# A hybrid decoder layer on one core: the second norm's row products moved from VectorE to ScalarE and GpSimd, its sums moved into PSUM banks

## The chip, the cores and the metric

One core of a Trainium2 chip runs the whole layer. TensorE (PE) multiplies into PSUM, VectorE (DVE), ScalarE (ACT) and GpSimd (POOL) work on tiles in SBUF and, the first two, in PSUM; SyncE (SP) issues most transfers. The metric is the device time of one launch in microseconds, as the median of several runs.

## The reference

The layer works on 1024 rows (the sequence) of 1024 float32 values. Cut to what matters here:

```
h  = rms_norm(x, mix_norm);  z = h @ w_in
o_gla = gated linear attention of part of z, RMS-normed per head and gated
o_swa = sliding-window attention with sinks of the rest of z
x  = x + concat([o_gla, o_swa]) @ w_out
h2 = rms_norm(x, ffn_norm)            # x * rsqrt(mean(x*x) + eps) * gain, row by row
u  = causal_dwconv(h2 @ w_up, conv_w, conv_b);  a, b = split(u)
out = x + (silu(a) * b) @ w_down
```

The change lies in the stretch from `@ w_out` to the first products of `h2 @ w_up`.

## The kernel before

**Numbers and products.** Float32 accuracy is had from a faster format: each operand is kept as a high part (rounded, `F32R`) and a low part (the value less the high part). `split` makes them: ScalarE copies the high part, GpSimd (or the engine named) subtracts. A product takes three passes, high by high, high by low, low by high, so a 128x512 output over 512 inner values is twelve matmuls.

**Seven products for eight.** Each large product is a 2x2 block product done in a Strassen-like scheme of seven block products P1 to P7 on sums and differences of blocks. Row tiles are 128 rows; tile `t` and tile `t + 4` are the upper and lower half of a block pair. Several products may go onto the same bank: `onto` in `o_product` says which. For `w_out`, P6, P5 and P3 go onto P1's bank, and after each the bank is added to a part of the residual rows `acc` (line 838, in `o_adds`, VectorE). P7 and P4 have banks of their own: P7 is added to both halves of `acc[i + 4]`, P4 to half 0 of it.

**Second norm.** When `acc[t]` is whole, after P3 for `t < 4` and after P4 for `t >= 4`, these steps follow:

- `norm2_stat(t)`: ScalarE squares `acc[t]` with a running sum (line 213). The squares themselves are not used; they are written into `h`, the buffer of the normed rows (`n2h`, two buffers). VectorE and GpSimd turn the sum into the row's factor `r` (lines 176 and 178).
- `norm2_rows(t)`: VectorE computes `h = acc * r * gain` in two halves (line 219).
- `norm2_tr(t)`: TensorE transposes `h` into two banks (eight 128x128 transposes). For `t < 4` (line 274, in `tr_hi`) ScalarE writes the high parts into `big`, a copy `b11` of the first half's transposes is kept, and low parts follow: the first half's on GpSimd from `b11` for `t < 3` (line 229), the rest on VectorE (line 286). For `t >= 4` (line 240) the banks are left to the next step.
- `norm2_sums(t)`, `t >= 4`: VectorE forms the differences and sums that the Strassen scheme of the next product wants: T1 = p0 - b11, T3 = p1 - b12, T2 = p1 + b11 (line 262, into the second half of `h`), T4 = b21 - T2 + ... (lines 264 and 265), each split into `big` or `ex[0..2]`. T2's low part goes to GpSimd, the others to VectorE.

**Order.** The program is a list of events, each with a time in units of about 5.2 us (`at`, `at_us`; `O` is the start of the `w_out` products, `TU` = `O` + 14 the start of the `w_up` products). Events are sorted by that time and issued. From `O` to `TU`, TensorE's order is fixed to be that of the list. On VectorE, ScalarE, GpSimd and SP the framework orders the instructions by priority and by its own estimate of when they are ready; each engine then works strictly in that order on the chip. The products of the last part run P2, P3, P4 for pair 0, then P2 and P3 for 1, P7 for 2, P4 for 1, and so on to P7 and P4 for pair 3; the transposes stand between them, at `O + 0.5 * n` for the tile's `n`.

**First chunks of the next product.** `w_up` is read in 22 chunks of channels with two sides each (`load_side`, into three `raw` buffers). Chunk 0's operands are split or summed during the stretch (`first_sums`, lines 910 to 918, VectorE), and also A11 and A12 of chunk 1. After tile 3's transposes come chunk 0's P1 and P2, tile 7's transposes, chunk 1's P1 and P2, then chunk 0's P3 (operand S4), P5 and P6. Chunk 1's other sums (lines 910 to 912) are on GpSimd.

**Gate transposes.** `gate_tr(7)` (line 667), the last of the linear attention's gated outputs, stands among the first `w_out` products.

Of the kernel before, what the change touches and what calls it, by code (L numbers as in the profile page):

```python
# [9 lines left out]
F32 = mybir.dt.float32  # L10
F32R = mybir.dt.float32r
I32 = mybir.dt.int32
AF = mybir.ActivationFunctionType
# [4 lines left out]
P = 128  # L18
T = 1024
D = 1024  # L20
NT = T // P
KD = D // P
# [6 lines left out]
SUMS, EA, EB = 2.01, -25, -14  # L29
# [5 lines left out]
def hymba_layer_kernel(ctx, tc, x, mix_norm, w_in, w_alpha2, b_alpha, gla_norm,  # L35
# [3 lines left out]
    act, dve, pool, pe, sp = nc.scalar, nc.vector, nc.gpsimd, nc.tensor, nc.sync  # L39
# [30 lines left out]
    def raw_tile(name):  # L70
        return base.tile([P, 1024], F32, tag="raw", name=name, bufs=RAW_BUFS)
# [109 lines left out]
    halves = (slice(0, 512), slice(512, D))  # L181
# [22 lines left out]
    def norm1(t):  # L204
        for i in range(2):
            norm1_mul(t, i)
        norm1_stat(t)

    def norm2_stat(t):
        pn, acc = fin["pn"], fin["acc"][t]  # L210
        h = fin["h", t] = pn.tile([P, D], F32, tag="n2h", name=f"n2h_{t}", bufs=2)
        ss = pn.tile([P, 1], F32, tag="n2ss", name=f"n2ss_{t}", bufs=2)
        act.activation(h, acc, AF.Square, accum_out=ss)
        fin["r", t] = rms_scale(ss, D, 1, f"n2{t}", pn, "n2")

    def norm2_rows(t):
        h, acc, r = fin["h", t], fin["acc"][t], fin["r", t]
        for c in halves:
            dve.scalar_tensor_tensor(h[:, c], acc[:, c], r[:, 0:1], fin["ffn"][:, c],  # L219
                                     op0=ALU.mult, op1=ALU.mult)  # L220

    def norm2_tr(t):
        h = fin["h", t]
        if t < 4:
            b11 = fin["b11"] = fin["pn"].tile([P, 4, 2, P // 2], F32, tag="b11", name=f"b11_{t}", bufs=1)
            tr_hi(t, 0, h, "n2", True)
            act.copy(b11, trs["n2", t, 0])
            if t < 3:
                pool.tensor_sub(tr_dst(t, 0, 1, True), b11, tr_dst(t, 0, 0, True).bitcast(F32))
            else:  # L230
                tr_lo(t, 0, "n2", True)
            tr_hi(t, 1, h, "n2", True)
            tr_lo(t, 1, "n2", True)
            return
        pbs = fin["pb", t] = []
        for q in range(2):
            pt = bank(f"n2pt_{t}_{q}")
            for k in range(4):
                c = (q * 4 + k) * P
                pe.transpose(pt[:, k * P:(k + 1) * P], h[:, c:c + P], ident)  # L240
            pbs.append(pt.rearrange("p (k c h) -> p k h c", k=4, h=2))

    def norm2_sums(t):

        i, ex = t - 4, fin["ex"]
        p0, p1 = fin["pb", t]

        def put(src, dst, eng=dve):
            dst = dst.rearrange("p k r (h c) -> p k r h c", h=2)
            split(src, dst[:, :, 0], dst[:, :, 1], eng)  # L250

        b12 = fin["h", t][:, 0:512].rearrange("p (k h c) -> p k h c", k=4, h=2)
        b11 = fin["b11"]
        b21 = big[:, i, 4:8].bitcast(F32).rearrange("p k r (h c) -> p k r h c", h=2)
        act.copy(b12, p0)
        put(p1, big[:, t, 4:8])
        dve.tensor_sub(p0, p0, b11)
        put(p0, big[:, t, 0:4])
        dve.tensor_sub(p1, p1, b12)
        put(p1, ex[1][:, i])  # L260
        t2 = fin["h", t][:, 512:].rearrange("p (k h c) -> p k h c", k=4, h=2)
        dve.tensor_add(t2, p1, b11)
        put(t2, ex[0][:, i], pool)
        dve.tensor_sub(p0, b21[:, :, 0], t2)
        dve.tensor_add(p0, p0, b21[:, :, 1])
        put(p0, ex[2][:, i])

# [12 lines left out]
    def tr_dst(t, q, r, parted):  # L280
        dst = big[:, t, q * 4:q * 4 + 4, r, :]
        return dst.rearrange("p k (h c) -> p k h c", h=2) if parted else dst

    def tr_lo(t, q, tag, parted=False):
        hi, lo = (tr_dst(t, q, r, parted) for r in range(2))
        dve.tensor_sub(lo, trs[tag, t, q], hi.bitcast(F32))
# [10 lines left out]
    raws = {}  # L297
# [366 lines left out]
    def gate_tr(t, gs):  # L664
        pb = bank(f"ogt{t}")
        for h in range(4):
            pe.transpose(pb[:, h * P:(h + 1) * P], gs[:, h * P:(h + 1) * P], ident)
        pv = pb.rearrange("p (h c) -> p h c", h=4)
        g32, l32 = (a[:, t, :].rearrange("p (j c) -> p j c", j=4) for a in (vg[0], qo))
        hi, lo = big[:, t, 0:4, 0, :], big[:, t, 0:4, 1, :]  # L670
        act.activation(hi, pv, AF.Copy, scale=glan)
        dve.scalar_tensor_tensor(lo, pv, glan, hi.bitcast(F32), op0=ALU.mult, op1=ALU.subtract)
        if t < 4:
            act.activation(g32, pv, AF.Copy, scale=glan)
            split(l32, big[:, t, 4:8, 0, :], big[:, t, 4:8, 1, :])
            return
        i = t - 4
        dve.scalar_tensor_tensor(pv, pv, glan, l32, op0=ALU.mult, op1=ALU.subtract)
        s2 = fin["ex"][1][:, (i + 2) % 4]
        split(pv, s2[:, :, 0], s2[:, :, 1], dve)  # L680
        split(l32, big[:, t, 4:8, 0, :], big[:, t, 4:8, 1, :])
        dve.tensor_add(qo[:, i, :], pb, qo[:, i, :])
        dve.tensor_sub(vg[0][:, i, :], vg[0][:, i, :], pb)
# [5 lines left out]
    fin = {}  # L689
# [60 lines left out]
    psb = {}  # L750
# [64 lines left out]
        sp.dma_start(fin["acc"][t], x[t * P:(t + 1) * P, :])  # L815

    def o_product(name, i):
        onto = "P1" if name in ("P6", "P5", "P3") else None
        if onto is None:
            psb["o", name, i] = bank(f"o{name}_{i}")  # L820
        pb = psb["o", onto or name, i]
        left = o_left(name, i)
        for k in range(4):
            for n, (ra, rb) in enumerate(PASSES):
                pe.matmul(pb, lhsT=left[:, k, ra, :], rhs=two_streams(ow[name, k][:, rb, :]),  # L825
                          start=(onto is None and k == 0 and n == 0), stop=(k == 3 and n == 2),
                          skip_group_check=onto is not None)

        if (name, i) not in (("P7", 0), ("P7", 1)):
            o_adds(name, i, pb)  # L830

    def o_adds(name, i, pb=None):
        if pb is None:
            pb = psb["o", name, i]
        for dt, half in {"P1": ((0, 0),), "P6": ((4, 0),), "P5": ((4, 1),), "P3": ((0, 1),), "P2": ((0, 0),),
                         "P7": ((4, 1), (4, 0)), "P4": ((4, 0),)}[name]:
            part = fin["acc"][i + dt][:, half * 512:half * 512 + 512].rearrange("p (h c) -> p h c", h=2)
            dve.tensor_add(part, part, halves_of(pb))
        if name in ("P3", "P4"):
            norm2_stat(i + 4 if name == "P4" else i)  # L840
# [52 lines left out]
        dve.tensor_copy(cc, pcc[:, 0:176].rearrange("p (a b) -> p a b", a=4))  # L893

    def load_side(ch, sd):
        raw = raws["u", ch, sd] = raw_tile(f"up{ch}_{sd}").rearrange("p (k n) -> p k n", k=KD)
        c0 = sd * DFF + ch * P
        sp.dma_start(raw, w_up[:, c0:c0 + P].rearrange("(k p) n -> p k n", p=P))

# [296 lines left out]
    def at(time, f, *a):  # L1196
        ev.append((time, len(ev), f, a))
# [45 lines left out]
    TQ, TK, TV, TG, TR, TO = 0.0, 8.0, 12.8, 20.8, 28.8, 36.8  # L1243
# [67 lines left out]
    for t in range(NT):  # L1311
        s = 11.0 + 1.9 * t
        at(s - (0.7 if t == 4 else 0.3), swa_qt, t)
        at(s + 1.0, swa_scores, t, 0)
        at(s + 1.6, swa_scores, t, 1)
        at(s + 3.2, swa_pt, t, 0)
        at(s + 3.8, swa_pt, t, 1)
        at(s + 4.9, swa_pv, t)
        s = TG + t
        at(s - 2.4, gla_lh, t)  # L1320
        at(s - 1.4, gla_exp, t)
        at(s + 1.0, gla_tr, t)
        if t < NT - 1:
            if t:
                at(s + 1.75, gla_mid, t + 1)
            at(s + 1.8, gla_state, t)
        at(s + 1.9, gla_a, t)
        at(s + 2.7, gla_o, t)
        at(TR + t + 1.3 if t < 7 else O + 0.75, lambda tt=t: gate_tr(tt, psb.pop(("r", tt))))
    at(TR + 2.0, open_acc)  # L1330
    for k2 in range(2):
        at(TR + 1.6 + 0.05 * k2, load_local, k2)
# [26 lines left out]
    for n, (name, i) in enumerate((("P2", 0), ("P3", 0), ("P4", 0), ("P2", 1), ("P3", 1), ("P7", 2), ("P4", 1), ("P2", 2),  # L1359
# [3 lines left out]
        if name in ("P3", "P4"):  # L1363
            t = i + 4 if name == "P4" else i
            at(u + 0.005, norm2_rows, t)
    for t, n in ((0, 19), (4, 20), (1, 22), (5, 24), (2, 26), (6, 27), (3, 28)):
        at(O + 0.5 * n - 0.002, norm2_tr, t)
        if t > 3:
            at(O + 0.5 * n + 0.01, norm2_sums, t)
    at(TU - 7.994, mark)  # L1370
    def at_us(us, f, *a):
        at(TU + us / 5.2, f, *a)
# [39 lines left out]
    at_us(1.8, open_ff)  # L1412
    at_us(starts[2, 0] - 0.05, open_down_banks)
    at_us(-42, load_chunk, 0)
    at_us(-41, load_side, 1, 0)
    for (ch, op), us in (((0, "A11"), EA), ((0, "A12"), EB), ((1, "A11"), -9.8), ((1, "A12"), -9.7),
                         ((0, "S4"), 1.74), ((0, "S1"), 1.75), ((0, "S2"), 1.77), ((0, "S3"), 1.9),
                         ((0, "A22"), 1.91)):
        at_us(us, *((behind,) if us < 0 and ch else ()), up_operand, ch, op)
# [73 lines left out]
```

## Time and profile before

| | us |
|---|---|
| runs: median (lowest to highest, 3 runs) | 999.76 (999.27 to 1000.34) |
| the profiled execution's own time | 1001.43 |
| its span, first to last instruction | 999.7 |
| TensorE busy | 974.2 |
| VectorE busy | 825.3 |
| GpSimd busy | 647.5 |
| ScalarE busy | 500.0 |

The span is what the profile's rows are measured in; the profiled execution is 1.7 us longer than its span and 0.17% above the median. A busy TensorE is not TensorE at its peak, as matmuls are pipelined. A wait on TensorE's row names the engine and line that released it. All times in rows are microseconds from the first instruction, unless a column is said to be nanoseconds.

### The profile page before, as it was taken

Reading aid. Unit: us, or ns where it says so; the run is one execution under the profiler, and the core shown is the slowest. Engines: PE = TensorE matmul, PEld = TensorE weight load, DVE = VectorE, ACT = ScalarE, POOL = GpSimd, SP = SyncE. Lnnn points to the kernel's source line nnn. Section 1 sums busy time; section 2 is a strip of 40 time slices with the busy share of each in tenths; the row PEclk is TensorE's granted clock in tenths of the full one; section 3 lists DMA queues with packets and bytes.
Section 4 is the critical chain, followed back from the end, with each engine's and each line's share of the span. In section 5 each row is a group of like instructions: output and inputs, shape, how many; then the busy total and the mean of one; then the engine's idle time right before and its main releaser. Section 6 shows DMA issues by size and latency. Waiting matters only on the chain.

```text
span 999.7 us, 13937 instructions
## 1 busy us (share of the span) xinstructions
PE 974.2 (97%) x4915; PEld 842.5 (84%) x4915; DVE 825.3 (83%) x1368; ACT 500.0 (50%) x1029; POOL 647.5 (65%) x539
## 2 busy tenths in 40 slices
PE   8999999999999978999999999999999999999998
PEld 6888887888888766878888888888888888888887
DVE  6877767767565798698999989898989899898986
ACT  5637655445454354455454545545454545455451
POOL 5592132335575424787879788887888788978750
PEclk9999999999999997999999999999999999999999
DMA  7152223131305101212121221212120212222104
GB/s 228 62 154 70 46 57 87 27 86 64 106 1 189 43 0 43 85 43 64 43 64 42 64 63 50 77 43 85 43 85 22 66 42 63 64 63 64 43 22 169
DMA packets 67541, 68.23 MB, mean 68 GB/s; under 512 B 4651, under 2 KB 52238, under 8 KB 67471
## 3 DMA queue, kind: packets, MB, share of 16 engines
q1 hardware_dynamic: 63484, 62.35, 20.4%
q10 hardware_dynamic: 3986, 4.99, 2.1%
q8 instruction: 39, 0.64, 0.3%
q14 instruction: 32, 0.25, 0.1%
HBM read 58.41 MB, written 4.19 MB: 63 GB/s over the span
## 4 chain that ended last, share of the span: by engine, by line
PE 77%; DVE 9%; POOL 5%; issue 3%; DMA 2%; ACT 2%; ACTq 0%; SPq 0%; POOLq 0%; DVEq 0%
PE fb L976 35%; PE dn_P L1157 17%; PE dg L348 4%; PE dr L348 4%; PE dv L348 3%; PE oP L825 3%; PE pv L534 1%; DVE n2h L219 1%; PE dl L1186 1%; PE fb L1186 1%; PE dq L848 1%; DMA up<-in_w_up_dram 1%; PE go L644 1%; PE ga L635 1%; DMA wob<-in_w_out_dram 1%
## 5 line engine op out<-in xcount | busy, mean ns | idle before, releaser
L1157 PE MATMUL dn_P<-dw,dg 128*128 128x512 f32 x840 | 205.2, 381 | 1.4 <-DVE acc L1161 0.7
L1161 DVE TENSOR_TENSOR acc<-acc,dn_P 128x1024 f32<-128x1024 f32 x140 | 169.3, 1210 | 31.3 <-PE dn_P L1157 31.2
L1157 PEld LDWEIGHTS dn_P<-dw,dg 128*128 128x128 f32 x840 | 157.2, 189 | 27.8 <-DVE acc L1161 3.2
L107 POOL TENSOR_TENSOR dw<-dn,dw 128x512 fp32r<-128x512 f32 x50 | 64.6, 1292 | 35.6 <-ACT dw L104 35.6
L983 DVE SCALAR_TENSOR_TENSOR ua<-fb,cc,ua 128x511 f32<-128x511 f32 (+1 forms) x84 | 61.9, 739 | 1.2 <-ACT ua L988 0.8
L976 PE MATMUL fb<-big,A11w 128*128 128x512 f32 x252 | 58.3, 380 | 1.1 <-ACT e L1032 1.1
L976 PE MATMUL fb<-big,S1w 128*128 128x512 f32 x252 | 58.6, 379 | 0.0
L976 PE MATMUL fb<-big,A12w 128*128 128x512 f32 x252 | 58.1, 379 | 0.0
L976 PE MATMUL fb<-big,S4w 128*128 128x512 f32 x252 | 58.1, 379 | 0.0
L976 PE MATMUL fb<-ex,S2w 128*128 128x512 f32 x252 | 58.0, 379 | 0.0
L976 PE MATMUL fb<-ex,S3w 128*128 128x512 f32 x252 | 57.8, 379 | 0.0
L976 PE MATMUL fb<-ex,A22w 128*128 128x512 f32 x252 | 57.8, 379 | 0.0
L510 POOL TENSOR_TENSOR pr<-pr,sm 128x512 f32<-128x512 f32 x16 | 17.3, 1080 | 61.4 <-DVE sm L509 36.0
L988 ACT ACTIVATE ua<-fb,cc 128x512 f32<-128x512 f32 x42 | 32.7, 778 | 46.6 <-DVE fb L1036 30.1
L976 PEld LDWEIGHTS fb<-big,A11w 128*128 128x128 f32 x252 | 47.5, 189 | 8.2 <-ACT e L1032 1.5
L976 PEld LDWEIGHTS fb<-big,A12w 128*128 128x128 f32 x252 | 47.6, 189 | 6.8
L976 PEld LDWEIGHTS fb<-ex,S2w 128*128 128x128 f32 x252 | 47.6, 189 | 6.8
L976 PEld LDWEIGHTS fb<-ex,S3w 128*128 128x128 f32 x252 | 47.6, 189 | 6.8
L976 PEld LDWEIGHTS fb<-big,S4w 128*128 128x128 f32 x252 | 47.6, 189 | 6.8
L976 PEld LDWEIGHTS fb<-ex,A22w 128*128 128x128 f32 x252 | 47.6, 189 | 6.8
L976 PEld LDWEIGHTS fb<-big,S1w 128*128 128x128 f32 x252 | 47.6, 189 | 6.8
L107 POOL TENSOR_TENSOR A22w<-up,A22w 128x512 fp32r<-128x512 f32 x22 | 30.0, 1364 | 31.6 <-ACT A22w L104 31.6
(487 smaller groups left out, 2571.8 us busy)
## 6 DMA issues: line engine op xcount, KB each, us to landing
up<-in_w_up_dram SPq DMA_DIRECT2D x44, 512.0 KB, 3.8
dn<-in_w_down_dram SPq DMA_DIRECT2D x22, 512.0 KB, 3.5
acc<-in_x_dram SPq DMA_DIRECT2D x8, 512.0 KB, 4.8
out_dram<-acc SPq DMA_DIRECT2D x15, 256.0 KB, 2.1
xt<-in_x_dram SPq DMA_DIRECT2D x7, 512.0 KB, 3.3
vraw<-in_w_in_dram SPq DMA_DIRECT2D x4, 512.0 KB, 3.9
graw<-in_w_in_dram SPq DMA_DIRECT2D x4, 512.0 KB, 4.0
qt<-qt ACTq DMA_DIRECT2D x16, 128.0 KB, 2.2
```

The costliest lines, as they stand in the source:

```text
L107: (eng or pool).tensor_sub(lo, src, hi.bitcast(F32))
L219: dve.scalar_tensor_tensor(h[:, c], acc[:, c], r[:, 0:1], fin["ffn"][:, c], op0=ALU.mult, op1=ALU.mult)
L348: pe.matmul(pb[:, :n], lhsT=big[:, t, k, ra, :], rhs=two_streams(ws[k][:, rb, :n]), start=(k == 0 and i == 0), stop=(k == KD - 1 and i == 2))
L510: pool.tensor_tensor(pr, pr, den[:, hs].rearrange("p (j o) -> p j o", o=1).broadcast_to((P, 4, P)), ALU.mult)
L534: pe.matmul(pbs[i][HALF[g]], lhsT=vv[rows, t - 1 + b, HALF[g]], rhs=rhs[rows, :, HALF[i]], start=start, stop=stop)
L825: pe.matmul(pb, lhsT=left[:, k, ra, :], rhs=two_streams(ow[name, k][:, rb, :]), start=(onto is None and k == 0 and n == 0), stop=(k == 3 a ...
L976: pe.matmul(pb, lhsT=w[:, ra, k, :], rhs=b_operand(bn, k, rb).rearrange("p t (h c) -> p t c h", h=2), start=(onto is None and i == 0), sto ...
L983: dve.scalar_tensor_tensor(dst, src, w, dst, op0=ALU.mult, op1=ALU.add)
L988: act.activation(u[:, a:z], y[:, a:z], AF.Identity, bias=b, scale=w2)
L1157: pe.matmul(pb[:, i], lhsT=g[:, ra, c:c + P], rhs=two_streams(w[:, rb, :]), start=(onto is None and n == 0), stop=(n == 2), skip_group_che ...
L1161: dve.tensor_add(acc, acc, pb.rearrange("p i (c h) -> p i h c", h=2))
L1186: pe.matmul(pb[:, c0:c1], lhsT=g[:, ra, (t % 4) * P:(t % 4 + 1) * P], rhs=two_streams(w[:, rb, c0:c1]), start=(ch == NCH - 2 and i == 0), ...
```

## The change

It has these parts:

- For tiles 0, 1, 2, 4 and 5, `norm2_rows` becomes a copy with the row factor on ScalarE and a product with the gain on GpSimd, each in two halves. Tiles 3, 6 and 7 stay on VectorE.
- For `t < 7` the squares go to a scratch, the `raw` buffer that later holds side 0 of chunk 1; `h` is taken only when the rows are computed. That load moves from `TU` - 41 us to `O + 13.01`, and the split of chunk 1's A11 and A12 from about -9.8 to -4.8 us before `TU`.
- The low part from `b11` for `t < 3` and T2's low part go from GpSimd to VectorE. T2 is formed in the bank p1 in place, not in `h`; the order within `norm2_sums` changes accordingly.
- For pairs 2 and 3, P4 goes onto P7's bank, and half 0 of `acc[i + 4]` gets one add in place of two.
- `gate_tr(7)` and the transposes of tiles 0 and 4 each stand one product later in TensorE's order.

```diff
+    def early_raw():
+        if "up1_0" not in fin:
+            fin["up1_0"] = raw_tile("up1_0")
+        return fin["up1_0"]
+
     def norm2_stat(t):
         pn, acc = fin["pn"], fin["acc"][t]
-        h = fin["h", t] = pn.tile([P, D], F32, tag="n2h", name=f"n2h_{t}", bufs=2)
         ss = pn.tile([P, 1], F32, tag="n2ss", name=f"n2ss_{t}", bufs=2)
-        act.activation(h, acc, AF.Square, accum_out=ss)
+        if t == 7:
+            fin["h", t] = pn.tile([P, D], F32, tag="n2h", name=f"n2h_{t}", bufs=2)
+        act.activation(fin["h", t] if t == 7 else early_raw(), acc, AF.Square, accum_out=ss)
         fin["r", t] = rms_scale(ss, D, 1, f"n2{t}", pn, "n2")
 
+    ROWS_POOL = (0, 1, 2, 4, 5)
+
     def norm2_rows(t):
-        h, acc, r = fin["h", t], fin["acc"][t], fin["r", t]
+        acc, r = fin["acc"][t], fin["r", t]
+        if t < 7:
+            fin["h", t] = fin["pn"].tile([P, D], F32, tag="n2h", name=f"n2h_{t}", bufs=2)
+        h = fin["h", t]
+        if t in ROWS_POOL:
+            for c in halves:
+                act.activation(h[:, c], acc[:, c], AF.Copy, scale=r[:, 0:1])
+                pool.tensor_mul(h[:, c], h[:, c], fin["ffn"][:, c])
+            return
         for c in halves:
             dve.scalar_tensor_tensor(h[:, c], acc[:, c], r[:, 0:1], fin["ffn"][:, c],
...
             act.copy(b11, trs["n2", t, 0])
-            if t < 3:
-                pool.tensor_sub(tr_dst(t, 0, 1, True), b11, tr_dst(t, 0, 0, True).bitcast(F32))
-            else:
-                tr_lo(t, 0, "n2", True)
+            tr_lo(t, 0, "n2", True)
...
         act.copy(b12, p0)
         put(p1, big[:, t, 4:8])
+        dve.tensor_sub(p1, p1, b12)
+        put(p1, ex[1][:, i])
         dve.tensor_sub(p0, p0, b11)
         put(p0, big[:, t, 0:4])
-        dve.tensor_sub(p1, p1, b12)
-        put(p1, ex[1][:, i])
-        t2 = fin["h", t][:, 512:].rearrange("p (k h c) -> p k h c", k=4, h=2)
-        dve.tensor_add(t2, p1, b11)
-        put(t2, ex[0][:, i], pool)
-        dve.tensor_sub(p0, b21[:, :, 0], t2)
+        dve.tensor_add(p1, p1, b11)
+        put(p1, ex[0][:, i])
+        dve.tensor_sub(p0, b21[:, :, 0], p1)
         dve.tensor_add(p0, p0, b21[:, :, 1])
         put(p0, ex[2][:, i])
...
-        onto = "P1" if name in ("P6", "P5", "P3") else None
+        onto = "P1" if name in ("P6", "P5", "P3") else "P7" if name == "P4" and i > 1 else None
...
+            if name == "P7" and i > 1 and half == 0:
+                continue
             part = fin["acc"][i + dt][:, half * 512:half * 512 + 512].rearrange("p (h c) -> p h c", h=2)
             dve.tensor_add(part, part, halves_of(pb))
...
-        raw = raws["u", ch, sd] = raw_tile(f"up{ch}_{sd}").rearrange("p (k n) -> p k n", k=KD)
+        raw = raws["u", ch, sd] = (early_raw() if (ch, sd) == (1, 0) else raw_tile(f"up{ch}_{sd}")).rearrange("p (k n) -> p k n", k=KD)
...
-        at(TR + t + 1.3 if t < 7 else O + 0.75, lambda tt=t: gate_tr(tt, psb.pop(("r", tt))))
+        at(TR + t + 1.3 if t < 7 else O + 1.25, lambda tt=t: gate_tr(tt, psb.pop(("r", tt))))
...
-    for t, n in ((0, 19), (4, 20), (1, 22), (5, 24), (2, 26), (6, 27), (3, 28)):
+    for t, n in ((0, 20), (4, 21), (1, 22), (5, 24), (2, 26), (6, 27), (3, 28)):
...
-    at_us(-41, load_side, 1, 0)
-    for (ch, op), us in (((0, "A11"), EA), ((0, "A12"), EB), ((1, "A11"), -9.8), ((1, "A12"), -9.7),
+    at(O + 13.01, load_side, 1, 0)
+    for (ch, op), us in (((0, "A11"), EA), ((0, "A12"), EB), ((1, "A11"), -4.8), ((1, "A12"), -4.7),
```

## The prediction

> **What bounds the kernel now.** I read the page's busy shares first, then who waited for whom on TensorE, then a table of busy time by stretch, then the order of TensorE's work in that stretch.
>
> ```profile
> PE 974.2 (97%) x4915; PEld 842.5 (84%) x4915; DVE 825.3 (83%) x1368; ACT 500.0 (50%) x1029; POOL 647.5 (65%) x539
> ```
>
> TensorE is busy for 97% of the span, so only 25 us can come from filling its gaps (the rest would need fewer or faster matmuls, and the change keeps every matmul). So the question is which gaps lie where the change is made. Waits on TensorE between 285 and 400 us (total, times, longest):
>
> ```profile
> PE n2pt L240 <- DVE n2h L219: 5.7, 4, 2.5
> PE fb L274 <- DVE n2h L219: 3.3, 1, 3.3
> PE n2pt L274 <- DVE n2h L219: 1.2, 1, 1.2
> PE ogt L667 <- POOL gs L661: 0.7, 1, 0.7
> PE oP L825 <- DVE acc L838: 0.6, 1, 0.6
> ```
>
> Three rows, 10.2 us, are the same thing: the second norm's transposes (lines 240 and 274) wait for VectorE's row products (line 219). With the bank wait of line 825 it is 10.8 us; the gate transpose adds 0.7. The stretch itself (TensorE, weight loads, VectorE, ScalarE, GpSimd busy, then granted clock):
>
> ```profile
> 350.00:360.00 10.00, 9.57 (x49) 8.10 (x47) 10.00 (x18) 5.11 (x10) 1.80 (x3) 1.00 0.00 1
> 360.00:370.00 10.00, 7.67 (x42) 6.54 (x43) 9.60 (x15) 5.67 (x10) 2.23 (x3) 1.00 0.00 0
> 376.00:382.00 6.00, 4.91 (x16) 3.73 (x16) 5.17 (x10) 3.98 (x8) 6.00 (x6) 0.72 0.08 22
> 382.00:386.00 4.00, 1.11 (x6) 1.14 (x7) 4.00 (x7) 0.62 (x1) 2.29 (x2) 0.76 0.80 231
> 386.00:392.00 6.00, 6.00 (x19) 4.84 (x19) 5.09 (x8) 3.55 (x7) 1.09 (x2) 0.59 0.00 1
> ```
>
> VectorE is full (10.00 and 9.60 of 10) while GpSimd works 1.80 and 2.23. And there is a second loss that no wait row shows: the clock falls to 0.72, 0.76, 0.59. Its price is busy time times the missing clock: 4.91 x 0.28 + 1.11 x 0.24 + 6.00 x 0.41 = 4.1 us. Where the gaps stand, in TensorE's order:
>
> ```profile
> 343.34 1.29 PE L274 MATMUL n2pt<-ident,n2h 128*128 128x128 f32 x8 [1.18 <-DVE n2h L219]
> 344.38 2.84 PE L825 MATMUL oP<-oP7w,big 128*128 128x512 f32 x12
> 347.05 1.28 PE L240 MATMUL n2pt<-ident,n2h 128*128 128x128 f32 x8
> 360.69 0.63 PE L240 MATMUL n2pt<-ident,n2h 128*128 128x128 f32 x4 [1.12 <-DVE n2h L219]
> 369.64 2.86 PE L825 MATMUL oP<-oP7w,big 128*128 128x512 f32 x12 [0.58 <-DVE acc L838]
> 374.98 0.63 PE L240 MATMUL n2pt<-ident,n2h 128*128 128x128 f32 x4 [2.49 <-DVE n2h L219]
> 376.66 0.63 PE L240 MATMUL n2pt<-ident,n2h 128*128 128x128 f32 x4 [1.05 <-DVE n2h L219]
> 384.89 1.94 PE L274 MATMUL fb<-ident,n2h 128*128 128x128 f32 x8 [3.33 <-DVE n2h L219]
> 386.65 4.94 PE L976 MATMUL gb<-big,A11w 128*128 128x512 f32 x12
> 394.81 2.84 PE L976 MATMUL fb<-big,A11w 128*128 128x512 f32 x12
> 400.08 2.75 PE L976 MATMUL gb<-big,S4w 128*128 128x512 f32 x12
> ```
>
> These are row tiles 0, 4, 5, 6, 3 (tile 5's second half waits 1.0 too: 5.7 less 1.12, 2.49 and 1.05). Waits near 1.1 us left the clock at 1.00 until 370; the waits of 2.49 and 3.33 us bracket the fall. The first product of channel chunk 0 then takes 4.94 us for twelve matmuls that take 2.84 at 394.81.
>
> **The change, part by part.** *Rows.* Two VectorE products per tile leave for tiles 0, 1, 2, 4 and 5. The groups of VectorE's work between 338 and 392 us, and its total from tile 0's statistic to the end of tile 3's rows:
>
> ```profile
> L219 DVE SCALAR_TENSOR_TENSOR n2h<-acc,n26r,ffn 128x512 f32<-128x512 f32 x2 | 3.4, 1716 | 0.0
> L219 DVE SCALAR_TENSOR_TENSOR n2h<-acc,n25r,ffn 128x512 f32<-128x512 f32 x2 | 3.0, 1529 | 0.0
> L219 DVE SCALAR_TENSOR_TENSOR n2h<-acc,n24r,ffn 128x512 f32<-128x512 f32 x2 | 2.4, 1260 | 0.1
> L265 DVE TENSOR_TENSOR n2pt<-n2pt,big 128x512 f32<-128x512 f32 x3 | 2.1, 695 | 0.0
> L219 DVE SCALAR_TENSOR_TENSOR n2h<-acc,n20r,ffn 128x512 f32<-128x512 f32 x2 | 1.4, 750 | 0.1
> 341.62:385.41 43.79, 32.94 (x162) 26.93 (x161) 40.78 (x66) 24.12 (x45) 18.54 (x18) 0.95 0.08 24
> ```
>
> Tiles 1 and 2 cost 1.4 like tile 0. Removed: 1.4 + 2.4 + 1.4 + 3.0 + 1.4 = 9.6 us. *Added to VectorE:* low parts of b11 (tiles 0 to 2) and of the T2 sum (tiles 4 to 6 here), six operations with an operand in a bank, 0.69 us long and 0.6 apart when they follow each other: +3.6. *P4 onto P7's bank* takes two adds out (tiles 6 and 7, half 0): -1.2. So 40.8 - 9.6 - 1.2 + 3.6 = 33.6 us of VectorE work remain to the end of tile 3's rows. Two more pieces may leave: the split of chunk 1's A11 and A12 (two operations, 1.2), which now waits for a later load, and the part of tile 6's sums that stands ahead of tile 3's rows (six, 3.6). And tile 6's rows fall from 3.4 to 1.4 if GpSimd leaves them alone. So 26.8 to 33.6; with the 3.0 us that VectorE idled there (43.79 - 40.78), tile 3's rows are ready at 371.4 to 378.2. I take the middle, 374.8.
>
> TensorE alone: the product before tile 0's transposes ended at 342.2 (343.34 less the gap of 1.18); nine products of 2.67 us (starts 344.38 to 347.05) and six transposes of 1.04 (343.34 to 344.38) end at 372.4. So VectorE leaves 2.4 us of waiting; with 0.8 for a new wait (below) that is 3.2 where 10.8 were: **-7.6 us**.
>
> *The new rows' own path.* Each now goes pow on GpSimd, two scaled copies on ScalarE, two products on GpSimd. No row of before does just that; the nearest are a 128x512 copy from SBUF on ScalarE and a 128x512 two-operand GpSimd instruction, alone and beside VectorE's SBUF work:
>
> ```profile
> 372.18 0.86 POOL L178 TENSOR_TENSOR n26r<-n26v,mhalf 128x1 f32<-128x1 f32 x1 [7.24 <-DVE n26v L176]
> 372.42 0.62 ACT L104 CAST A22w<-up 128x512 fp32r<-128x512 f32 x1
> 373.02 1.27 POOL L107 TENSOR_TENSOR S4w<-up,S4w 128x512 fp32r<-128x512 f32 x1
> 373.15 3.36 DVE L219 SCALAR_TENSOR_TENSOR n2h<-acc,n26r,ffn 128x512 f32<-128x512 f32 x2
> 374.24 1.72 POOL L107 TENSOR_TENSOR ex<-n2h,ex 128x512 fp32r<-128x512 f32 x1
> 376.44 0.69 DVE L265 TENSOR_TENSOR n2pt<-n2pt,big 128x512 f32<-128x512 f32 x1
> ```
>
> Latency from the statistic: 0.6 + 0.6 + 2 x 1.27 = 3.7 us, up to 0.86 + 0.62 + 2 x 1.72 = 4.9, against 1.4 to 3.0 before. I take 3.7, since the VectorE operations left are mostly of the bank form (line 265, 0.69 under a busy GpSimd). GpSimd gains ten products (12.7 to 17.2 us) and loses six subtractions of 1.27 to 1.72 here (7.6 to 10.3). With its 18.54 us that is 21 to 28 in 33: not full. ScalarE gains ten copies (6.2 us) on 24.1: not full. The cover for the longer latency is TensorE's order: tiles 0 and 4 go one product (2.6 us) later, and the statistic no longer waits for a norm buffer, as Square writes a scratch. For tile 0: statistic at 341.62 (where the window above begins), products done 3.7 and a queue step later, some 345.6, and TensorE there at 342.2 + 2.67 = 344.9: at most 0.7 us, which I count within the 2.4, as a wait here delays everything behind it alike. Uncovered, one tile costs 3.7.
>
> *P4 onto P7's bank* makes TensorE's second P4 (tile 7) wait until VectorE has added P7's other half; tile 6's transposes (1.04) stand between. VectorE's queue decides: nothing if it is free, up to three queued operations of 0.6 beyond the transposes otherwise, so 0 to 1.8; I take 0.8. P7's bank is held longer; the bank wait of 0.58 goes, as fewer banks are opened, or returns in tile 6's transposes: 0.6 either way, taken as nothing.
>
> *The clock.* With 3.2 us spread over four places near 1 us each, the waits are like those that left the clock at 1.00: **-4.1**; if one wait above 2.5 us stays, about half returns.
>
> *Gate transpose one product later*: its gate product was 0.7 us late and gets 2.6: **-0.7**. What it frees (tile 7's left operands, two differences) is first read products later: nothing; uncovered, 0.7 again.
>
> *Chunk 1's first load* moves behind the last use of the scratch, tile 3's Square (before the rows of tile 3 at 374.8, so by some 372). It stands on SP's queue ahead of two more loads of this kind, which went out at 380 before and so do not wait for it:
>
> ```profile
> 380.15 1.60 SPq L898 DMA_DIRECT2D up<-in_w_up_dram  x2
> 399.90 1.28 POOL L107 TENSOR_TENSOR ex<-n2h,ex 128x512 fp32r<-128x512 f32 x1 [10.69 <-ACT ex L104]
> 401.13 1.29 POOL L910 TENSOR_TENSOR S<-up 128x512 f32<-128x512 f32 x1
> 407.85 2.75 PE L976 MATMUL fb<-ex,S2w 128*128 128x512 f32 x12
> 430.51 2.86 PE L976 MATMUL fb<-big,A11w 128*128 128x512 f32 x12 [1.10 <-ACT e L1032]
> up<-in_w_up_dram SPq DMA_DIRECT2D x44, 512.0 KB, 3.8
> ```
>
> Landing takes 3.8 us, the split 0.6 + 0.7 for each half: ready by 379. TensorE wants it at the chunk's first product, 394.81 before and about 382 after: nothing, with 3 us of cover. If the split sits on ScalarE's queue ahead of tile 3's cast, it costs 1 to 2.
>
> *Afterwards.* TensorE reaches the products of line 976 at 400.08 some 11.7 us earlier. GpSimd's sums for chunk 1 (401.13) must follow: they stood behind tile 7's T2 low part, for which GpSimd idled 10.69 us and which now goes to VectorE; their data was on its way at 380. So they can start near 385: nothing lost, and the wait at 430.51 (1.1 us) bounds the further gain.
>
> **Sum.** 7.6 + 4.1 + 0.7 = 12.4 us. The profiled execution took 1001.43 us beside its span of 999.7; the runs' median, 999.76, is 0.17% below it. Against the profile 989.0, against the median **987.4**.
>
> **Rivals.** *VectorE still paces it.* Its queue keeps tile 6's sums in front and tile 6's rows stay slow: 33.6 + 3.0 puts tile 3's rows at 378.2. TensorE then waits 5.8 + 0.8 of the 10.8, and at least half the clock loss stays: 4.2 + 2.0 + 0.7 = 6.9, time 992.9. For it: VectorE at 93% before (40.78 of 43.79), and 33.6 of work against TensorE's 24.0 + 6.2. Against it: two SBUF operands were the slow form, and most of those leave.
>
> A second road to this rival: GpSimd's ten products now run where VectorE's remaining two-SBUF operations run (four row halves of tiles 6 and 3, two splits). The rows at 373.15 (two in 3.36, 1.4 alone) show each waiting about a microsecond: 6 x 1.0 more on VectorE, 374.8 becomes 380.8, the waits 9.2, the gain 1.6 + 2.0 + 0.7 = 4.3, time 995.5. The Trainium skill, SBUF — State Buffer, "Practical consequences", says that a VectorE instruction with two SBUF inputs contends with a GpSimd instruction that reads SBUF and that the later one fully blocks; the 1716 ns mean at tile 6 beside 0.69 for the bank form agrees. By its rule a row half would be up to 0.75 + 1.27 = 2.0 us, an estimate, where the trace has 1.77 at most.
>
> *Slower: the new row path is exposed.* At each of five tiles TensorE arrives before the factor is there and waits the whole 3.7 us: 18.5, and 3.3 for tile 3, against 10.8, less the 0.7 of the gate; the clock loss stays or doubles (0 to 4.1, I take 2). Time 999.8 + 10.3 + 2 = 1012. It decides, with the clock loss staying, when more than 1.6 us of each path is exposed (5 x 1.64 + 3.3 = 10.8 + 0.7). The factor comes from VectorE's queue, which is freer, so that speaks against it: tile 0 exposes 0.5.
>
> *No change: the next stage is paced by GpSimd.* If its sums for chunk 1 started at 401.13 as before, TensorE would wait at 407.85's product and all but 1 us would be given back: 999. Only a late load does that, and it was issued at 380 before.
>
> **How the numbers follow.** The forecast's chance is 0.60, its own range 983 (all waits gone: 12.4 + 3.2 + 1.1 = 16.7) to 990. VectorE pacing, by either road, 0.22, 990 to 996. No change 0.06. Slower 0.12. Two runs of this kernel can be told apart from about 0.2%, 2 us. The range is 983 to 996: 0.82 of the chance. Faster by over 0.2%: 0.60 + 0.22 + little = 0.83; same 0.06; slower 0.11.
>
> **What the new profile would show.** Right: transposes of lines 240 and 274 waiting under 4 us in all, the clock at 1.00 through the stretch, the first product of line 976 near 375 and in about 2.8 us. Rows products on GpSimd near 1.3 us, VectorE's bank forms at 0.69. GpSimd's first chunk sum ahead of TensorE's S4 product. Wrong: a new wait of transposes for GpSimd's rows, of line 825 for the P7 add, or a clock below 0.8 after it.

## The result: 0.6% slower, and the profile after

| | before | after |
|---|---|---|
| median of five runs, us | 999.76 (998.35 to 1000.75) | 1005.88 (1002.86 to 1007.64) |
| ratio, 95% interval | | 1.006, 1.0039 to 1.0082 |
| span of the profiled execution, us | 999.7 | 1005.1 |
| VectorE / ScalarE / GpSimd busy, us | 825.3 / 500.0 / 647.5 | 818.4 / 505.8 / 649.2 |

The forecast was 987.4, faster. VectorE did get 7 us of work less, and TensorE's waits are where the loss must be read. Who TensorE waited for in the kernel after (whole span, total, times, longest; rows outside the changed stretch and rows under 1 us left out):

```profile
PE gb L990 <- DVE big L298: 6.3, 1, 6.3
PE oP L837 <- DVE vg L695: 4.9, 1, 4.9
...
PE fb L286 <- DVE n2h L235: 1.6, 1, 1.6
...
PE n2pt L286 <- POOL n2h L232: 1.6, 2, 1.1
PE n2pt L253 <- DVE n2pt L276: 1.3, 2, 0.8
```

The waits for rows, 10.2 us before, are down to 1.6 + 1.6 + 0.2 for VectorE and GpSimd together (the 0.2 is a wait of line 253 for GpSimd). But two new waits stand above them, 6.3 and 4.9 us, and neither is a wait for a row. TensorE's order in the kernel after shows where:

```profile
288.23 0.60 PE L679 MATMUL ogt<-ident,gs 128*128 128x128 f32 x4
288.59 8.02 PE L837 MATMUL oP<-ex,big 128*128 128x512 f32 x36
296.44 0.60 PE L679 MATMUL ogt<-ident,gs 128*128 128x128 f32 x4
301.90 5.46 PE L837 MATMUL oP<-ex,big 128*128 128x512 f32 x12 [4.86 <-DVE vg L695]
...
342.58 2.75 PE L837 MATMUL oP<-oP2w,big 128*128 128x512 f32 x12
...
384.27 1.32 PE L286 MATMUL fb<-ident,n2h 128*128 128x128 f32 x8 [1.64 <-DVE n2h L235]
385.61 1.99 PE L990 MATMUL gb<-big,A11w 128*128 128x512 f32 x8
393.94 2.07 PE L990 MATMUL gb<-big,A11w 128*128 128x512 f32 x4 [6.34 <-DVE big L298]
395.81 4.76 PE L990 MATMUL gb<-big,A12w 128*128 128x512 f32 x12
400.40 1.04 PE L253 MATMUL fb<-ident,n2h 128*128 128x128 f32 x8
```

The same marks in the kernel before: tile 6's gate transpose at 290.40, P2 of pair 1 at 336.82, chunk 0's first product at 386.65, tile 7's transposes at 394.02. So, from mark to mark:

| piece | before | after | difference |
|---|---|---|---|
| gate transpose 6 to P2 of pair 1 | 46.4 | 54.4 | **+7.9** |
| P2 of pair 1 to chunk 0's first product | 49.8 | 43.0 | **-6.8** |
| that product to tile 7's transposes | 7.4 | 14.8 | **+7.4** |

The norm's stretch gained 6.8 us, where the forecast has 9.2 up to there: 7.6 of waits, and the 1.6 of the clock loss that lies ahead of the first product (4.91 x 0.28 + 1.11 x 0.24). It was lost twice over: once 40 us earlier, behind the gate transpose, and once right after it, inside the first product. The three differences add up to 8.5 us and the two spans differ by 5.4, because two smaller pieces go the other way. Tile 6's gate transpose already starts 2.2 us earlier in this trace, ahead of the changed stretch (in the fourteen traces of this case it starts anywhere from 288.2 to 290.9), and 1.0 us comes back after tile 7's transposes.

Both waits brought a slow clock with them. Busy times of TensorE, weight loads, VectorE, ScalarE, GpSimd, then the granted clock, in the kernel after, in the 10.7 us behind the first wait and from the first product to tile 7's transposes:

```profile
301.90:312.60 10.70, 10.70 (x36) 8.92 (x37) 4.05 (x5) 3.61 (x6) 2.55 (x2) 0.73 0.22 73
385.60:400.40 14.80, 8.46 (x24) 6.54 (x25) 9.45 (x13) 3.83 (x7) 4.99 (x4) 0.65 0.04 10
```

By the prediction's arithmetic that is 10.70 x 0.27 = 2.9 us and 8.46 x 0.35 = 3.0 us, so the waits cost 7.8 and 9.3 us in all. The second is more than the +7.4 of the table, as the kernel before lost 2.1 us to the clock in that piece too (4.94 for the first product instead of 2.84).

### The profile page after: what moved, and what is told of

It is laid out like the page before. It is cut to its first block, busy times and chain, and to the rows that moved or that the text cites. A ratio compares the mean times of both kernels' runs of the same rounds, so it can differ in the third digit from the quotient of the medians.

```text
span 1005.1 us, 13939 instructions
## 1 busy us (share of the span) xinstructions
PE 975.3 (97%) x4915; PEld 842.7 (84%) x4915; DVE 818.4 (81%) x1363; ACT 505.8 (50%) x1039; POOL 649.2 (65%) x542
## 4 chain that ended last, share of the span: by engine, by line
PE 55%; DVE 5%; POOL 2%; issue 1%; DMA 0%; ACT 0%; POOLq 0%; ACTq 0%
PE fb L990 35%; PE dn_P L1171 17%; PE dl L1200 1%; PE fb L1200 1%; DVE n2h L235 1%; PE gb L990 1%; DVE acc L1175 1%; DVE ua L997 0%; DVE ex L107 0%; DMA up<-in_w_up_dram 0%; POOL dw L107 0%; DVE acc L852 0%; DVE big L107 0%; DVE big L298 0%; ACT ex L104 0%
```

## The experiments

All times are medians, and each ratio is against runs of the kernel before on the same chip.

**1. The gate transpose's bank.** The banks of PSUM are taken from two pools of four. A product of `w_out` named P1 always comes from pool a, where its four banks are held until P3 has been added. The other products of `w_out` and the second norm's transposes have a pool fixed by name too. All other names, the gate transposes among them, take the pools in turn, by a counter of the banks taken. Tile 7's gate transpose was the 205th bank (pool b); moved behind one more product it is the 206th, in pool a, beside three P1 banks. The fourth P1 must then wait until the last reader of the gate's bank is through, which is line 695 on VectorE:

```profile
297.80 0.75 DVE L684 SCALAR_TENSOR_TENSOR big<-ogt,glan,big 128x512 fp32r<-128x512 f32 x1 [0.47 <-ACT big L683]
298.47 0.75 DVE L690 SCALAR_TENSOR_TENSOR ogt<-ogt,glan,qo 128x512 f32<-128x512 f32 x1
299.87 0.69 DVE L107 TENSOR_TENSOR ex<-ogt,ex 128x512 fp32r<-128x512 f32 x1 [0.65 <-ACT ex L104]
300.48 0.68 DVE L694 TENSOR_TENSOR qo<-ogt,qo 128x512 f32<-128x512 f32 x1
301.07 0.68 DVE L695 TENSOR_TENSOR vg<-vg,ogt 128x512 f32<-128x512 f32 x1
```

This is VectorE of the kernel after in order of time: five operations on the transposed gate, two of them behind ScalarE; when the last has ended at 301.75, TensorE's product of 301.90 starts (shown above). To test it, only the pool of that one bank was changed:

```diff
-                              ("b", ("oP", "n2pt"))):
+                              ("b", ("oP", "n2pt", "ogt7"))):
```

> The changed kernel, with the bank of gate transpose 7 taken from the other PSUM pool (the one that does not hold P1's four banks); its later place is kept. Theory A (the later place changes the parity by which banks alternate, so that the transpose lands among P1's four banks and the fourth P1 product waits until VectorE has read that bank): the wait of 4.86 us before 301.90 and the low clock after it go, 997 to 999 against 1005.9. Rival (the fourth P1 product waits for the gate's data or VectorE's queue, whatever the bank): no change, 1004 to 1007.

Measured: 999.4, ratio 0.9991 (0.9982 to 0.9999). The 4.86 us row is gone, and the clock of 300 to 340 us is 1.00 where it was 0.91. The time is 0.4 us above theory A's range, but the wait and the clock loss went as it says; the rival falls. The other direction, the old kernel with the gate transpose moved and nothing else:

```diff
-        at(TR + t + 1.3 if t < 7 else O + 0.75, lambda ...)
+        at(TR + t + 1.3 if t < 7 else O + 1.25, lambda ...)
```

> The kernel before, with gate transpose 7 one product later and nothing else. Theory A: the wait of about 4.9 us and the clock loss of about 3.4 us appear, less the 0.7 us that the transpose waited before: 1006 to 1009. Rival (the wait needs the rest of the change): 999 to 1000.

Measured: 1006.11, ratio 1.006 (1.0047 to 1.0072). One line, moved by one product, costs as much as the whole change lost. And the same line with the bank in pool b:

> The kernel before, with gate transpose 7 one product later and its bank in the pool without P1's banks. Theory A: the wait of 0.7 us goes and nothing comes: 998.5 to 1000 beside 999.8 to 1000.2 for the kernel before. Rival (the later place costs something besides the bank): above 1001.

Measured: 997.55, ratio 0.998 (0.9968 to 0.9991): the later place is a small gain, as intended, once the bank is right. It came out 1 us below the range, and the 0.7 us wait does not explain that. In its trace the norm's waits are no shorter (4.1 us before tile 3's transposes, 3.3 in the kernel before), but the granted clock between 340 and 390 is 0.97 where the kernel before has 0.91. Why the clock differs there is not shown.

**2. The low part of tile 3.** The first product of chunk 0 runs its eight matmuls on high parts, then stands still for the low part of tile 3's first half (line 298). VectorE's queue in the kernel after:

```profile
386.00 0.68 DVE L107 TENSOR_TENSOR A12w<-up,A12w 128x512 fp32r<-128x512 f32 x1
386.61 0.68 DVE L107 TENSOR_TENSOR ex<-n2pt,ex 128x512 fp32r<-128x512 f32 x1
387.21 0.68 DVE L274 TENSOR_TENSOR n2pt<-n2pt,b 128x512 f32<-128x512 f32 x1
387.81 0.14 DVE L176 TENSOR_SCALAR n27v<-n2ss 128x1 f32<-128x1 f32 x1
387.87 0.68 DVE L298 TENSOR_TENSOR big<-fb,big 128x512 fp32r<-128x512 f32 x1
388.68 3.41 DVE L235 SCALAR_TENSOR_TENSOR n2h<-acc,n27r,ffn 128x512 f32<-128x512 f32 x2
392.01 0.68 DVE L107 TENSOR_TENSOR ex<-n2pt,ex 128x512 fp32r<-128x512 f32 x1
392.61 0.68 DVE L276 TENSOR_TENSOR n2pt<-big,n2pt 128x512 f32<-128x512 f32 x1
393.21 0.68 DVE L298 TENSOR_TENSOR big<-fb,big 128x512 fp32r<-128x512 f32 x1
```

Two low parts (line 298) with tile 7's rows between them: the one at 387.87 is the second half's; the first half's, which TensorE wants first, comes at 393.21. A chain through `b11` stands ahead of it. There is one `b11` buffer. Tile 3's copy into it must wait for the last reader of tile 2's, which is tile 6's T2 sum (line 274, 387.21; before, the sum ran at 383.40). In the program the low part stands after the copy, and both read the same bank. That the framework keeps the two in this order is inferred; part 3 tests it by swapping them. ScalarE in the kernel after:

```profile
387.92 0.59 ACT L104 CAST ex<-n2pt 128x512 fp32r<-128x512 f32 x1 [0.74 <-DVE n2pt L274]
388.41 0.59 ACT L243 COPY b<-fb 128x512 f32<-128x512 f32 x1
```

Tile 7's rows stand ahead of the low part in VectorE's order, presumably because by the framework's estimate their factor was ready before the copy was. They took 3.41 us, not the 1.40 of before (389.44 in the old trace), while GpSimd ran chunk 1's sums beside them. Test: keep everything, but order tile 7's rows behind that low part.

```diff
-            at(u + 0.005, norm2_rows, t)
+            if t == 7:
+                at(O + 13.9985, rows_behind_lo, t)
+            else:
+                at(u + 0.005, norm2_rows, t)
```

Here `rows_behind_lo` is `norm2_rows` with its VectorE instructions ordered after tile 3's first low part.

> The changed kernel, with tile 7's rows on VectorE ordered behind the low part of tile 3's first half. Theory B (the first product of channel chunk 0 stands still for 6.3 us because that low part is queued behind tile 7's rows, which take 3.4 us beside GpSimd's sums): the wait falls to 2 to 3 us and half of the clock loss goes, 1000 to 1003 against 1005.9. Rival (the low part is late because ScalarE's copy of the same bank comes late, VectorE's queue does not matter): at most 1 us, 1004 to 1006.

Measured: 1000.77, ratio 1.0009 (0.9998 to 1.0019). The wait is 2.9 us, not 6.3, and 5 us are back against the kernel after. Both readings had a part in it: the queue was the larger, and 2.0 of the 2.9 us that are left go when the copy of `b11` is out of the way (part 3, where 0.9 stays).

**3. Both repaired.** The copy drops out if the low part is formed ahead of it:

```diff
+            if t == 3:
+                tr_lo(t, 0, "n2", True)
             act.copy(b11, trs["n2", t, 0])
-            tr_lo(t, 0, "n2", True)
+            if t < 3:
+                tr_lo(t, 0, "n2", True)
```

With this and the bank in pool b:

> The changed kernel with both repaired: gate transpose 7 in the other pool, and tile 3's first low part formed ahead of ScalarE's copy of that bank (so it no longer waits for the copy, nor stands behind tile 7's rows). If A and B are the two losses and they add up: 998 less 6 to 8, so 990 to 992. Rival (VectorE has no room, another of its operations becomes late in place of this one): 994 to 998.

Measured: **991.25, ratio 0.9912 (0.9898 to 0.9926)**, faster than both kernels. TensorE at the two places, in the repaired kernel:

```profile
298.22 0.60 PE L682 MATMUL ogt<-ident,gs 128*128 128x128 f32 x4
298.57 2.84 PE L840 MATMUL oP<-ex,big 128*128 128x512 f32 x12
...
377.62 1.32 PE L289 MATMUL fb<-ident,n2h 128*128 128x128 f32 x8 [1.64 <-DVE n2h L235]
378.95 1.99 PE L993 MATMUL gb<-big,A11w 128*128 128x512 f32 x8
381.88 1.13 PE L993 MATMUL gb<-big,A11w 128*128 128x512 f32 x4 [0.93 <-DVE n27v L176]
382.84 2.75 PE L993 MATMUL gb<-big,A12w 128*128 128x512 f32 x12
```

The wait inside the first product is 0.93 us and the next product runs at full clock (2.75). (The row names tile 7's statistic; the low part itself ended beside it, at 381.82.) A control, the old kernel with the same swap of copy and low part:

> The kernel before, with tile 3's first low part formed ahead of ScalarE's copy of that bank, as in the second repair. Theory (there the low part was never late, so the repair only takes back a loss that the change brought): 999 to 1000.5, no difference. Rival (the repair is a gain by itself that the change had nothing to do with): 994 to 997.

Measured: 999.42, ratio 0.9996 (0.9986 to 1.0006). There it does nothing; the repair undoes a loss of the change.

**4. What the parts are worth.** From the repaired kernel, one part undone at a time. Rows back on VectorE (`ROWS_POOL = ()`):

> The kernel with both repairs (991.25 us), with all rows of the second norm back on VectorE. Theory C (the rows taken off VectorE are what shortens the norm's stretch): VectorE gets 9 to 10 us back in a stretch where it is nearly full, the waits of the transposes and the low clock return, 996 to 1001. Rival (the moved sums, the later transposes of tiles 0 and 4 and the scratch for the squares do it): 990 to 993.

Measured: 994.77, ratio 0.9947 (0.9932 to 0.9963). So 3.5 us of the gain are the rows, by the two ratios; neither reading alone is right. The busy times of its norm stretch (columns as above):

```profile
340.00:390.00 50.00, 41.62 (x204) 34.86 (x203) 47.44 (x78) 29.31 (x55) 16.19 (x16) 0.93 0.11 32
```

And whom TensorE waits for there:

```profile
PE n2pt L256 <- DVE big L301: 3.0, 1, 3.0
PE gb L993 <- DVE big L301: 2.4, 1, 2.4
PE oP L840 <- DVE big L301: 1.7, 1, 1.7
```

VectorE is full again (47.44 of 50) and its low parts, which now carry all that GpSimd did, are late. So the sums on VectorE need the room that the rows leave. The reverse is not so, as the next run shows.

Sums back on GpSimd (T2 in SBUF, low parts of T2 and `b11` on GpSimd):

> The kernel with both repairs, with T2 formed in SBUF again and its low parts and b11's on GpSimd (the rest of the new order of the sums is kept). Theory C (only the rows matter, VectorE has room for the six low parts): 990 to 993. Rival D (GpSimd, which now has the rows, stalls behind ScalarE's casts of T2 and delays rows and the next chunk's sums): 994 to 999. A third reading (the T2 sum in the bank keeps the bank too long and costs the 1.3 us of waits seen at line 276): 988 to 990.

Measured: 992.36, ratio 0.9928 (0.9912 to 0.9945): as theory C has it, the place of the sums makes no difference that shows, and the rows' move does not need it. P4 in banks of its own:

> The kernel with both repairs, with P4 of pairs 2 and 3 in banks of its own and both adds of P7 again. Theory C: VectorE does two adds more (1.2 us), the wait of the last P4 for the P7 add (0.5 us) goes: 990 to 993, not to be told from 991.25. Rival (the longer hold of P7's bank is what makes tile 6's transposes wait): 988 to 990; or the two adds do cost their time in a full VectorE: 992.5 to 994.

Measured: 994.64, ratio 0.9938 (0.9921 to 0.9956), which overlaps the repaired kernel's interval (up to 0.9926). TensorE in its trace, at the same place as above:

```profile
377.19 1.32 PE L289 MATMUL fb<-ident,n2h 128*128 128x128 f32 x8 [3.45 <-DVE n2h L235]
378.52 1.99 PE L991 MATMUL gb<-big,A11w 128*128 128x512 f32 x8
```

The wait of tile 3's transposes for VectorE's rows is 3.45 us instead of 1.64, as when the two adds cost their time, and yet the clock stayed at 1.00. This trace is of the shortest of the six runs, 991.26 us. The four at 994.5 us and above have a mean granted clock of 0.995 or 0.996 where this one has 1.000, so the median of 994.64 probably holds a clock loss that the trace does not show. What this part is worth is not settled.

**5. Attempts at the rest.** Tile 6's sums ordered behind tile 3's rows on VectorE, tile 7's rows on ScalarE and GpSimd, and both together:

> The kernel with both repairs, with tile 6's sums on VectorE ordered behind tile 3's rows. Theory E (of the forecast's VectorE work the part of tile 6's sums ahead of tile 3's rows is a real wait, 1.6 us before tile 3's transposes): that wait goes, 989 to 990.5 beside 991.25. Rival (VectorE is full, so what is moved back is late for the next product): 991 to 993.

Measured: 993.89, ratio 0.9947 (0.9934 to 0.9959), worse. The wait before tile 3's transposes grew to 2.29 us. VectorE in that run:

```profile
376.53 0.70 DVE L107 TENSOR_TENSOR A11w<-up,A11w 128x512 fp32r<-128x512 f32 x1 [1.48 <-ACT A11w L104]
377.15 1.40 DVE L235 SCALAR_TENSOR_TENSOR n2h<-acc,n23r,ffn 128x512 f32<-128x512 f32 x2
```

and TensorE behind it:

```profile
377.95 1.32 PE L298 MATMUL fb<-ident,n2h 128*128 128x128 f32 x8 [2.29 <-DVE n2h L235]
379.28 4.54 PE L1002 MATMUL gb<-big,A11w 128*128 128x512 f32 x12
```

With the sums gone from in front, the split of chunk 1's A11 stands there, and it waits for the load that the change moved late. Both theories are missed: the sums had only filled that wait. The first product took 4.54 us, so the clock was low there too; the next run shows that this does not need the longer wait.

> The kernel with both repairs, with tile 7's rows also on ScalarE and GpSimd. In the repaired kernel TensorE does not wait for tile 7's rows (no such row), so theory C says 990.5 to 992, no difference. Rival (VectorE's rows beside GpSimd's sums, 2.5 to 3.4 us for two, still cost): 988 to 990.

Measured: 992.55, ratio 0.9925 (0.9912 to 0.9938): 0.5 us above the range of theory C, and its interval overlaps the repaired kernel's, so no difference shows for work that nobody waits for. Its trace does differ at one place:

```profile
376.92 1.32 PE L289 MATMUL fb<-ident,n2h 128*128 128x128 f32 x8 [1.64 <-DVE n2h L235]
378.26 4.54 PE L993 MATMUL gb<-big,A11w 128*128 128x512 f32 x12
```

The wait is the repaired kernel's, 1.64 us, and the first product takes 4.54 us all the same, at a granted clock of 0.62.

> The kernel with both repairs, tile 6's sums behind tile 3's rows, and tile 7's rows on ScalarE and GpSimd. Theory E with C: 989 to 990.5, like the run with tile 3's rows first. Rival: with VectorE freed at both places the waits go together, 987 to 989.

Measured: 992.8, ratio 0.9932 (0.9919 to 0.9945): no gain, and both readings are missed; its wait before tile 3's transposes is 2.3 us too.

## Why the prediction was wrong

**The step that failed first is the gate transpose.** It was costed at -0.7, "uncovered, 0.7 again": only its data were followed. Its bank was not, although the counter and the two pools are in the code. Alone it costs 5.9 us (1006.11 against 1000.19 on that chip), a swing of 6.6 against the forecast. The later place, with its bank right, gives -2.2 (0.9 to 3.2 by the interval), of which 0.7 was forecast.

**The second is what comes after the stretch.** The prediction followed TensorE to tile 3's rows and took the first product from there at full speed. That product needs not only the rows' transposes but the low part, one step further down VectorE's queue. Chunk 0's operand, `b11` and tile 7's rows were each costed as hidden; nobody asked in which order VectorE's queue would hold them. The product stood still for 6.34 us there and its piece ran at a clock of 0.65. Repairing it brought 999.4 to 991.25.

**The middle was right in mechanism, and its gain was forecast too large.** VectorE's work to the end of tile 3's rows was forecast as 26.8 to 33.6 us with 3.0 us of idling. Busy times of the same piece in the kernel after:

```profile
347.26:384.88 37.62, 31.94 (x164) 25.76 (x162) 29.61 (x53) 29.44 (x54) 23.13 (x22) 1.00 0.12 33
```

and whom VectorE waited for in the norm's stretch (three of the rows):

```profile
DVE n21v L176 <- ACT up L219: 3.1, 1, 3.1
DVE big L298 <- ACT big L290: 2.2, 2, 1.7
DVE n24v L176 <- ACT up L219: 1.9, 1, 1.9
```

The work was 29.61, inside the range. The idling was 8.0 us (37.62 less 29.61), and this is the term that was too small. Most of it is in these rows: VectorE's next statistic stands in order behind ScalarE's Square, and ScalarE does the Square of one tile after the row copies of another. So the rows of tile 3 ended 37.6 us after tile 0's statistic where 33.2 was forecast, and TensorE's waits were 5.5 us there, not 3.2 (1.6 + 1.6 + 1.3 + 0.5 + 0.3 + 0.2): -5.3 in place of -7.6.

**The smaller steps.** GpSimd's row products took 1.33 us (1.27 taken) and ScalarE's scaled copies 0.72 (0.62 taken). The wait for the P7 add was 0.53, within its 0 to 1.8. A bank hold that the prediction did not name is the row `PE n2pt L253 <- DVE n2pt L276`, 1.3 us: with T2 in the bank, a transpose bank is free only when line 276 has read it (the hold that was taken as nothing was that of P7's bank). With T2 in SBUF again (part 4) that row is gone, a wait of 1.1 us for ScalarE stands at the same transposes, and the time did not get better (992.36). Chunk 1's late load did not hold TensorE in the kernel after, but it stood in the way of the reordering in part 5. GpSimd's sums of chunk 1 did come early, at 388.61 as against TensorE's S4 product at 406.46, as forecast.

**The rivals.** None of them is what happened. The slower one put the loss on the rows' longer path; the measured waits for GpSimd's rows are 1.8 us in all, so that its direction came true is luck. The second road, VectorE's rows slowed beside GpSimd, did happen, but at tile 7's rows (3.41 for two, 1.40 before), where it was not looked for. The clock term came true in part in the kernel after: up to the first product, with waits of 1.6 us at most, the clock stayed at 1.00, which is 1.6 of the 4.1 us. The other 2.5 were the first product's own (6.00 x 0.41), and there the clock was 0.65. That short waits keep the clock is not a safe rule: part 5 has the same wait of 1.64 us with the clock low behind it. With both losses repaired the kernel is at 991.25, a gain of 8.9 against the 1000.19 of that chip, where 12.4 was forecast. That lies within the range given, but it is a kernel other than the one that was forecast. Of the 8.9 the gate's place is some 2 and the rows 3.5; how the rest divides over the other parts is not shown.

## What to carry to other kernels

Moving an operation in TensorE's order also moves it in whatever hands out the banks; look up which bank it gets, and who must have read that bank before the next product may write it. Follow a gain to the instruction that TensorE needs next and then to the one behind that: a stretch that becomes shorter makes the order of the next engine's queue matter, and the order was planned for another timing. When a change has several parts and the total is bad, read the trace from mark to mark before judging any part; here the part that the change was named for worked.

## What the runs showed of the hardware that was not expected

The length of the one wait ahead of a product did not decide whether the clock fell. Before tile 3's transposes TensorE waited 3.45 us with P4 in banks of its own, and the first product ran at a granted clock of 1.00. It waited 2.29 us with tile 3's rows first, and the twelve matmuls took 4.54 us. It waited 1.64 us both in the repaired kernel, which kept the clock, and with tile 7's rows on GpSimd, where the product took 4.54 us too. Each of these is one profiled execution. The wait of 4.86 us left 0.73 over the next 10.7 us. The Trainium skill, TensorE: Matmul & The Clock Gate, "What's actually happening", has the clock at half after an idle window of about 3.4 us that runs freely. The 4.86 us wait agrees; the 3.45 us wait need not contradict it, as a window that runs freely seldom falls wholly into a wait of its own length. The falls after 2.29 and 1.64 us it does not explain, and what sufficed there is not shown.

VectorE's two row products of tile 7 took 3.41 us beside GpSimd's sums and 1.40 before, when GpSimd idled; the sums in banks stayed at 0.68 beside the same GpSimd. The Trainium skill, SBUF — State Buffer, "Practical consequences", says that a VectorE instruction with two SBUF inputs contends with a GpSimd instruction that reads SBUF, and that one with at most one SBUF input does not, outside VectorE's 2-port modes; both numbers agree.
